# Two-layer decoder trunk: causal masks by GpSimd selects in two of three B groups, four output weights loaded during B, output projection in two halves, compact reciprocals

## The chip, the cores and the metric

The kernel runs on one core of a Trainium2 chip. TensorE (PE) multiplies, VectorE (DVE), ScalarE (ACT) and GpSimd (POOL) do the element-wise work, and DMA queues that SyncE (SP) and ACT issue move data. Each engine works through its own list of instructions in a fixed order; a scheduler wrote these lists when the program was built. The metric is the device time of one launch in microseconds (us).

## The reference

1024 prompt tokens and 32 sample tokens (8 sequences of 4) pass two layers of width 1024 in float32.

- Layer 0: one input projection gives queries, keys and values of an attention A (window 128) and of three dilated attentions B (groups g = 1, 2, 3 with window and dilation (128, 1), (512, 4), (2048, 16)), with 8 query heads on 2 key heads (`kv` = 0, 1), and a gate z. The three B groups share one softmax denominator. The result is `[A | B] * silu(z)`, then an output projection (1024 to 1024), the residual and a LayerNorm.
- Layer 1: mLSTM with 4 heads of 256, computed in chunks of 128 tokens, a gate, an output projection of the same kind, the residual and a LayerNorm.

```python
s = jnp.where(mask, s, NEG_INF)
p = jnp.exp(s - m[..., None]);  den = p.sum(-1)          # m, den joint over the three B groups
o = jnp.einsum('nbhgqk,nbkhd->nbqhgd', p, vv) / den
mix = concat([oa, ob]) * silu(z);  y = mix @ w_out       # 8 blocks of 128 input features, k = 0..7
out = layer_norm(DN_ALPHA * x + y, ln_g, ln_b)
```

## The kernel before

Every float32 product is made of three matmuls of rounded parts (high by high, high by low, low by high), so splits into a high part (ACT, `hi`) and a low part (DVE, `lo`) stand everywhere. The stages are: keys and values; queries woven with attention A and the maxima of B; the gate; **stage B** (`attention_b`, `samples`, `merges`, woven by `weave`); the output projection of layer 0 (`out0`, `out_proj`); layer 1 (`layer1`), which ends with the same `out_proj`.

In stage B, `scores` goes through blocks of 128 keys by 4 heads x 128 queries. A block of B is six matmuls of 512 columns before the change: the mask (identity times mask, `maskr`), two for the scores (`sc`), and three for the values (`av`: twice `ph`, once `pl`). ACT takes the exponential of `sc` twice, rounded (`ph`) and whole (`p`). `lo` makes `pl = p - ph`, on DVE, or on POOL for every fourth block (`POOL_LO`). For each kv there are 8 blocks of g = 3, then 12 of g = 2, then 15 of g = 1. When the last group has finished the queries of a chunk (`CH`: 384, 384 and 256 + 32 tokens), `OD` (65 rows: 64 values and the denominator) goes to DRAM.

`merge0(ty, kv, c)` reads it back, divides by the denominator, multiplies by the gate and splits into `M[c]` (`mh`, `ml`), the left side of the output projection: (0, 0) and (0, 1) are A and fill feature blocks k = 0 to 3, (1, 0) fills 4 and 5, (1, 1) fills 6 and 7. For (1, 1), which is the last, it reads the bare denominators to 64 partitions each and takes the reciprocal there (line 839); for the others `finish` has stored reciprocals.

The weights `wo0` come through the two `wraw` buffers (`load_wo`: load, `hi`, `lo`): k = 0, 1 at the end of `samples`, k = 2 to 7 in `out0`. The matmuls of the output projection are lines 163 to 165 (`py`).

Of the kernel before, what the change touches and what calls it, by code (L numbers as in the profile page):

```python
# [66 lines left out]
POOL_LO = 4  # L67

# [5 lines left out]
class Scratch:  # L74


    def __init__(self, *tiles):
        self.free = [[t, 0] for t in tiles]
        self.tags = {}

# [15 lines left out]
class Builder:  # L96
# [57 lines left out]
    def proj_tok(self, ps, i, X, xs, w):  # L154


        nc = self.nc
        for k in range(8):
# [289 lines left out]
    def scores(self, g, kv, hf, Q1, Q2, K1, K2, V, emit):  # L448
        nc = self.nc
        for qb in range(2 * hf, 2 * hf + 2):  # L450
# [4 lines left out]
            for bi, (kb, kind) in enumerate(bl):  # L455
# [11 lines left out]
                if g:  # L467
                    nc.scalar.activation(ph, sc, AF.Exp)
                    nc.scalar.activation(p, sc, AF.Exp)  # L469
                else:  # L470
                    nc.scalar.activation(p, sc, AF.Exp)
                    nc.gpsimd.affine_select(p, p, [[0, 4], [-1 if kind else 1, 128]], OP.is_ge, 0.0, base=0,
                                            channel_multiplier=1 if kind else -1)
                    self.hi(ph, p)
                pl = self.ppool.tile([128, 512], F32R, tag="pl", name="pl")
                if g and self.nsc % POOL_LO == 0:
                    nc.gpsimd.tensor_tensor(pl, p, f(ph), OP.subtract)
                else:
                    self.lo(pl, p, ph)
# [21 lines left out]
    def finish(self, ty, kv, sink_nm=None):  # L501
# [10 lines left out]
        self.store('m', self.FD[ty][kv].rearrange("h (b q) -> (h b) q", q=128), dn)  # L512

# [48 lines left out]
    def attn_b(self, kv, done=None):  # L562
# [253 lines left out]
    def merge0(self, ty, kv, c, M, inverse=True):  # L816
# [10 lines left out]
        OD = self.OD[ty][kv]  # L827
        D = self.FD[ty][kv] if inverse else OD[64]
        for u in range(2 * ty):
            pr = slice(64 * u, 64 * u + 64)  # L830
            self.load(o[pr, :, :m], OD[0:64].rearrange("d (c u) t -> d c u t", u=2)[:, :, u, t0:t0 + m])
            self.load(F[pr, :, :m], D.rearrange("(c u) t -> c u t", u=2)[:, u, t0:t0 + m].partition_broadcast(64))
# [29 lines left out]
    def out_proj(self, M, W, xres, g, b, consume, early={}):  # L862
        nc = self.nc
        with self.tc.tile_pool(name="lnp", bufs=3) as lp:
            for i in ORDER:
                m = 128 if i < 8 else 32
                if i == 6:
                    xs = self.pair(lp, M[2])
                xr = None
                if i in early:  # L870
                    r = early[i]
                else:
                    xr = lp.tile([128, 1024], F32, tag="xr", name="xr")
                    r = [xr[:, 0:512], xr[:, 512:1024]]
                    self.load(xr[:m], xres[128 * i:128 * i + m])
                for n in range(2):
                    ps = self.pp.tile([128, 512], F32, tag=("pj", "sc")[n], name="py")
                    ns = slice(512 * n, 512 * n + 512)
                    self.proj_tok(ps, i, M, xs if i == 8 else None, lambda k: [w[:, ns] for w in W[k]])
                    nc.vector.scalar_tensor_tensor(r[n][:m], r[n][:m], ALPHA, ps[:m], op0=OP.mult, op1=OP.add)  # L880
                    for c in (32,) if i == 8 else ():
                        nc.vector.tensor_tensor(r[n][:32], ps[c:c + 32], r[n][:32], OP.add)
                self.layer_norm(m, r, g, b)
                consume(i, m, r, xr)

    def layer0(self):
# [13 lines left out]
        self.FD = [[dt(f"FD{t}{i}", [4, TP]) for i in range(2)] for t in range(2)]  # L900
        self.SZ = dt("SZ", [8, 128, T])
# [9 lines left out]
        with tc.tile_pool(name="qp", bufs=2) as self.qp, tc.tile_pool(name="kp", bufs=2) as self.kp, \  # L911
# [46 lines left out]
            def last(c):  # L958
                if c < 2:
                    self.merge0(1, 1, c, self.M, False)  # L960
# [32 lines left out]
            def samples():  # L993
                sp = Scratch(*(self.x2p.tile([128, 3072], F32, tag=f"x{u}x2", name=f"scr{u}") for u in "hl"))
# [10 lines left out]
            self.merge0(1, 1, 2, M, False)  # L1005
# [3 lines left out]
    def out0(self):  # L1009
        nc, tc, A = self.nc, self.tc, self.A  # L1010
        M = self.M
        self.mp.release()
        with tc.tile_pool(name="wo", bufs=1) as wp:
            W = self.W0 + [self.load_wo(A['wo0'], k, *self.wo_tiles(wp, k)) for k in range(2, 8)]
            with tc.tile_pool(name="lnc", bufs=1) as lc:
                gb = [[lc.tile([128, 512], F32, name=f"ln{u}{c}") for c in range(2)] for u in "gb"]
                self.load_ln(0, gb)
                tags = (("x2", self.x2p), ("0", self.xp), ("1", self.xp))
# [142 lines left out]
    def proj_head(self, h):  # L1161
# [3 lines left out]
        else:  # L1165
            QT = self.hp.tile([128, 2, T], F32, tag="QT", name="QT", bufs=1)
        KT = self.hp.tile([128, 2, T], F32, tag="KTh", name="KTh")
# [201 lines left out]
    def layer1(self):  # L1369
# [3 lines left out]
        with tc.tile_pool(name="l1c", bufs=1) as lc:  # L1373
# [16 lines left out]
            with tc.tile_pool(name="hp", bufs=2) as self.hp:  # L1390
# [5 lines left out]
                with tc.tile_pool(name="ms", bufs=2) as self.ms:  # L1396
# [11 lines left out]
                    def load_m(c):  # L1408
                        tg, pool = (("x2", self.x2p), ("0", self.xp), ("2", self.xp))[c]
# [13 lines left out]
                    for k, t in ((2, "KTh"), (3, "QT")):  # L1423
                        x = self.hp.tile([128, 2, 1024], F32R, tag=t, name=f"o{k}", bufs=2 if k == 2 else 1)
# [51 lines left out]
    def body(self):  # L1476
        nc, tc = self.nc, self.tc
        with tc.tile_pool(name="dram", bufs=1, space=DRAM) as self.dram, \
# [20 lines left out]
            self.x2p.release()  # L1499

# [137 lines left out]
```

## Time and profile before

| | us |
|---|---|
| median of 3 runs | 1497.02 (1495.68 to 1500.87) |
| the profiled execution, whole | 1504.22 |
| its span in the profile | 1501.9 |
| PE busy in the span | 1416.9 (94%) |
| DVE, ACT, POOL busy | 896.6, 514.3, 203.1 |
| mean granted clock of PE in the span | 0.979 |

Times below are from the span's start. Stage B runs from about 485 to 656, the output projection of layer 0 to 765, and layer 1 follows. Matmuls are pipelined, so the distance between the starts of two of them tells what one costs, not its duration.

### The profile page before, as it was taken

The numbers are of one execution on the slowest core, as the hardware profiler recorded it, in microseconds if no ns is written. First come the engines' busy times: TensorE is split into PE (matmuls) and PEld (weight loads), VectorE is DVE, ScalarE is ACT, GpSimd is POOL, SyncE is SP. The second block draws the span as 40 slices with busy tenths as digits, with TensorE's granted clock in tenths as the row PEclk, the third lists the DMA queues.
The fourth block names the chain that finished last, engine by engine and source line by source line (L and its number), as shares of the span: only waits on it lengthen the run. The fifth ranks groups of instructions, "written<-read, shape, count | busy, mean of one in ns | idle before, by whom it ended". The sixth has DMA issues, their size and how long they took to land.

```text
span 1501.9 us, 22033 instructions
## 1 busy us (share of the span) xinstructions
PE 1416.9 (94%) x7862; PEld 1203.8 (80%) x7862; DVE 896.6 (60%) x2480; ACT 514.3 (34%) x939; POOL 203.1 (14%) x249
## 2 busy tenths in 40 slices
PE   8999999998899898879999999999999999998997
PEld 8989999898898544457788878988898899877785
DVE  5312457577576756669774535655565566566786
ACT  5332254542123756721133313331333133333310
POOL 1002243422321212101000000100000000000010
PEclk9999999999999989989999999999999999999999
DMA  8446565556753789564222655364323322341741
GB/s 297 168 143 196 176 194 163 173 160 178 198 172 98 234 254 246 171 200 122 96 79 76 216 198 204 105 194 131 77 78 117 117 49 69 117 129 23 241 138 46
DMA packets 139306, 226.85 MB, mean 151 GB/s; under 512 B 17216, under 2 KB 107296, under 8 KB 138680
## 3 DMA queue, kind: packets, MB, share of 16 engines
q1 hardware_dynamic: 129496, 201.96, 44.0%
q10 hardware_dynamic: 9702, 23.50, 4.5%
q8 instruction: 62, 1.02, 0.3%
q14 instruction: 46, 0.38, 0.1%
HBM read 166.60 MB, written 81.88 MB: 165 GB/s over the span
## 4 chain that ended last, share of the span: by engine, by line
PE 69%; DMA 16%; DVE 8%; issue 4%; ACT 2%; SPq 1%; POOL 0%; DVEq 0%; ACTq 0%; POOLq 0%
PE pj L197 10%; PE pj L199 10%; PE pj L198 10%; PE py L163 3%; PE py L165 3%; PE py L164 3%; PE pvo L163 3%; PE pvo L164 3%; PE pvo L165 3%; DMA G<-GR 2%; DMA OD<-OD 1%; DMA K<-KK 1%; PE st L431 1%; DMA wr<-in_wo_dram 1%; DMA out_cmems_dram<-Cs 1%
## 5 line engine op out<-in xcount | busy, mean ns | idle before, releaser
L197 PE MATMUL pj<-xh,wh 128*128 128x384 f32 (+1 forms) x576 | 189.1, 328 | 8.4 <-DVE sz L609 3.3
L197 PE MATMUL pj<-x1h,wh 128*128 128x384 f32 (+1 forms) x576 | 189.3, 329 | 1.7 <-ACT QT L1171 1.6
L199 PE MATMUL pj<-xh,wl 128*128 128x384 f32 (+1 forms) x576 | 188.4, 327 | 0.0
L198 PE MATMUL pj<-xl,wh 128*128 128x384 f32 (+1 forms) x576 | 188.3, 327 | 0.0
L199 PE MATMUL pj<-x1h,wl 128*128 128x384 f32 (+1 forms) x576 | 187.6, 326 | 0.0
L198 PE MATMUL pj<-x1l,wh 128*128 128x384 f32 (+1 forms) x576 | 187.3, 325 | 0.0
L197 PEld LDWEIGHTS pj<-xh,wh 128*128 128x128 f32 x576 | 110.4, 192 | 12.6 <-DVE sz L609 4.3
L197 PEld LDWEIGHTS pj<-x1h,wh 128*128 128x128 f32 x576 | 108.3, 188 | 6.5 <-issue 3.3
L199 PEld LDWEIGHTS pj<-x1h,wl 128*128 128x128 f32 x576 | 108.3, 188 | 6.0 <-issue 5.8
L198 PEld LDWEIGHTS pj<-x1l,wh 128*128 128x128 f32 x576 | 108.4, 188 | 4.0 <-issue 3.8
L198 PEld LDWEIGHTS pj<-xl,wh 128*128 128x128 f32 x576 | 110.3, 191 | 1.6
L199 PEld LDWEIGHTS pj<-xh,wl 128*128 128x128 f32 x576 | 110.3, 192 | 0.9
L435 DVE CUSTOM_DVE_ANT_0 junk<-st,maskr 128x256 f32<-128x256 f32 (+1 forms) x256 | 93.0, 363 | 26.7 <-PE st L431 9.5
L163 PE MATMUL pvo<-voh,x1h 128*128 128x512 f32 x256 | 102.3, 402 | 3.0 <-DVE SZ L1187 3.0
L164 PE MATMUL pvo<-voh,x1l 128*128 128x512 f32 x256 | 101.4, 399 | 0.0
L165 PE MATMUL pvo<-vol,x1h 128*128 128x512 f32 x256 | 100.6, 396 | 0.0
L808 POOL TENSOR_TENSOR rsw<-rsw,mhalf 128x1 f32<-128x1 f32 (+1 forms) x54 | 40.1, 743 | 318.7 <-DVE rsw L807 303.5
L114 DVE TENSOR_TENSOR pl<-p,ph 128x512 fp32r<-128x512 f32 x82 | 63.6, 782 | 29.0 <-ACT p L469 16.6
L110 ACT ACTIVATE wh<-wr 128x1024 fp32r<-128x1024 f32 x48 | 50.7, 1057 | 75.9 <-PE pj L198 69.9
L120 POOL TENSOR_TENSOR wl<-wr,wh 128x1024 fp32r<-128x1024 f32 x24 | 58.0, 2415 | 131.1 <-ACT qs L231 70.6
L431 PE MATMUL st<-K,QZ 128*128 128x256 f32 x256 | 52.1, 292 | 10.7 <-DMA QZ<-QQ 5.6
L163 PEld LDWEIGHTS pvo<-voh,x1h 128*128 128x128 f32 x256 | 48.8, 191 | 13.8 <-DVE SZ L1187 3.3
(352 smaller groups left out, 3165.1 us busy)
## 6 DMA issues: line engine op xcount, KB each, us to landing
Q<-QQ SPq DMA_DIRECT2D x32, 512.0 KB
out_kvs_dram<-in_cache_b_kv_dram SPq DMA_DIRECT2D x16, 1022.0 KB
wr<-in_w0f_dram SPq DMA_DIRECT2D x24, 512.0 KB
wr<-in_w1f_dram SPq DMA_DIRECT2D x24, 512.0 KB
QQ<-sh ACTq DMA_DIRECT2D x16, 512.0 KB
QQ<-sl ACTq DMA_DIRECT2D x16, 512.0 KB
QZ<-QQ SPq DMA_DIRECT2D x32, 256.0 KB
wr<-in_wo_dram SPq DMA_DIRECT2D x16, 512.0 KB
```

What stands on the lines that cost most here:

```text
L110: return self.nc.scalar.activation(out, in_, AF.Copy, scale=scale)
L114: return self.nc.vector.tensor_tensor(out, in_, f(hi), OP.subtract)
L120: self.nc.gpsimd.tensor_tensor(out, in_, f(hi), OP.subtract)
L163: nc.tensor.matmul(ps, xh[:, k, t], wh, start=k == 0, stop=False)
L164: nc.tensor.matmul(ps, xl[:, k, t], wh, start=False, stop=False)
L165: nc.tensor.matmul(ps, xh[:, k, t], wl, start=False, stop=k == 7)
L197: nc.tensor.matmul(ps[:, :n], wh[:, k, :], xh[:, k, :n], start=k == 0, stop=False)
L198: nc.tensor.matmul(ps[:, :n], wh[:, k, :], xl[:, k, :n], start=False, stop=False)
L199: nc.tensor.matmul(ps[:, :n], wl[:, k, :], xh[:, k, :n], start=False, stop=k == 7)
L431: nc.tensor.matmul(st[:, u, :], Q1[:, h, q0:q0 + 128], K1[:, w0:w0 + 256], start=True, stop=True)
L435: nc.vector.tensor_tensor_reduce(junk[:, :n], st[:, u, c0:c0 + n], mk, 1.0, -3e38, OP.add, OP.max, ST[:, 8 * h + qb:8 * h + qb + 1])
L808: nc.gpsimd.tensor_tensor(r, v, self.mhalf[:m], OP.pow)
```

## The change

In g = 1 and g = 2 the mask matmul goes; POOL zeroes the masked half after the exponential (`affine_select`, as attention A does already), and ACT copies the result to `ph`. `POOL_LO` goes, so every `pl` is made on DVE. For (1, 1) a new `finish_chunk` loads the denominators of a chunk as 12 (or 8) rows of 128, takes the reciprocal there, stores it (`FDC`), and `merge0` reads that back and multiplies on POOL as for the others. `samples` loads four output weights instead of two, the new ones into the buffers that it has finished with, and some tiles of layer 1 move with these buffers. `out_proj` gives the first two token tiles their PSUM together and contracts k = 0 to 3 of both ahead of k = 4 to 7.

```diff
@@ scores
-                if g:
-                    mk = self.maskr[:, 256:384] if g == 3 else self.maskr[:, 128 - 128 * kind:256 - 128 * kind]
-                    nc.tensor.matmul(so, mk, self.identr.unsqueeze(1).to_broadcast([128, 4, 128]), start=True, stop=False)
-                nc.tensor.matmul(so, K1[:, ks], Q1[:, :, q0:q0 + 128], start=not g, stop=False)
+                if g == 3:
+                    nc.tensor.matmul(so, self.maskr[:, 256:384], self.identr.unsqueeze(1).to_broadcast([128, 4, 128]), start=True, stop=False)
+                nc.tensor.matmul(so, K1[:, ks], Q1[:, :, q0:q0 + 128], start=g < 3, stop=False)
...
-                if g:
+                if g == 3:
                     nc.scalar.activation(ph, sc, AF.Exp)
                     nc.scalar.activation(p, sc, AF.Exp)
                 else:
...
-                if g and self.nsc % POOL_LO == 0:
-                    nc.gpsimd.tensor_tensor(pl, p, f(ph), OP.subtract)
-                else:
-                    self.lo(pl, p, ph)
+                self.lo(pl, p, ph)
@@ new
+    def finish_chunk(self, c):
+        n = 4 * (min(CH[c][1], TP - CH[c][0]) // 128)
+        dn = self.mp.tile([128, 2, 384], F32, tag="mf", name="dnc")[:, 0, 0:128]
+        self.store('m', dn[:n], self.ODC[c][64].rearrange("h (b q) -> (h b) q", q=128))
+        self.nc.vector.reciprocal(dn[:n], dn[:n])
+        self.store('m', self.FDC[c].rearrange("h (b q) -> (h b) q", q=128), dn[:n])
@@ attn_b
-                    self.store('b', self.OD[1][kv][:, :, t], OD[:, :, t])
+                    self.store('b', self.ODC[qb // 3] if kv else self.OD[1][kv][:, :, t], OD[:, :, t])
@@ merge0
-            if inverse:
-                nc.gpsimd.tensor_tensor(o[:, :, :m], o[:, :, :m], F[:, :, :m], OP.mult)
-            else:
-                for a in range(2):
-                    nc.vector.reciprocal(F[:, a, :m], F[:, a, :m])
-                nc.vector.tensor_tensor(o[:, :, :m], o[:, :, :m], F[:, :, :m], OP.mult)
+            nc.gpsimd.tensor_tensor(o[:, :, :m], o[:, :, :m], F[:, :, :m], OP.mult)
@@ out_proj
-            for i in ORDER:
+            for grp in (ORDER[:2],) + tuple((i,) for i in ORDER[2:]):
+                parts = (range(4), range(4, 8)) if len(grp) > 1 else (range(8),)
...
@@ samples
-                for k in range(2):
-                    w = [self.wsp.tile([128, 1024], F32R, tag=f"w{u}", name=f"o{u}") for u in "hl"]
+                for k in range(4):
+                    if k < 2:
+                        w = [self.wsp.tile([128, 1024], F32R, tag=f"w{u}", name=f"o{u}") for u in "hl"]
+                    else:
+                        x = self.x2p.tile([128, 2, 1024], F32R, tag=f"x{'bc'[k - 2]}", name="ox")
+                        w = [x[:, 0, :], x[:, 1, :]]
```

What the scheduler makes of it shows at three places. First PE, near the end of stage B (g = 1, kv = 1). The number after a name is its buffer, and rises from block to block; `av` with `ph_6346` is the first value matmul of the block whose scores went to the `sc` before 6376.

```order
L462 MATMUL sc_6376<-identr_951,maskr_949 128x512
L463 MATMUL sc_6376<-Q1_6370,K1_6140 128x512
L464 MATMUL sc_6376<-Q2_6372,K2_6141 128x512
L483 MATMUL av_6327<-pl_6336,V_6146 66x512
L481 MATMUL av_6327<-ph_6346,V_6146 66x512
L482 MATMUL av_6327<-ph_6346,V_6146 64x512
```

That is the order before, where the values of a block come right behind the scores of the next one. The order of the changed kernel at the same place:

```order
L465 MATMUL sc_6387<-Q1_6381,K1_6147 128x512
L466 MATMUL sc_6387<-Q2_6383,K2_6148 128x512
L485 MATMUL av_6308<-pl_6317,V_6153 66x512
L483 MATMUL av_6308<-ph_6326,V_6153 66x512
L484 MATMUL av_6308<-ph_6326,V_6153 64x512
```

Here `ph_6326` belongs to the scores `sc_6322`; `sc_6337`, `sc_6350` and `sc_6387` stand between them and these values, so PE has two to three further blocks scored where it had one.

Second DVE, at the first reciprocal for (1, 1), chunk 0. `av_6202` holds the last queries of chunk 0; two more sums into `OD` stand between it and line 839, which works on 128 rows (`x2` is two of them):

```order
L576 TENSOR_TENSOR OD_5661<-av_6202,OD_5661 65x4x128
L114 TENSOR_TENSOR pl_6308<-p_6304,ph_6305 128x512
L576 TENSOR_TENSOR OD_5661<-av_6245,OD_5661 65x4x128
L114 TENSOR_TENSOR pl_6321<-p_6317,ph_6318 128x512
L114 TENSOR_TENSOR pl_6336<-p_6332,ph_6333 128x512
L576 TENSOR_TENSOR OD_5661<-av_6299,OD_5661 65x4x128
L839 RECIPROCAL mf_6232<-mf_6232 128x384 x2
L114 TENSOR_TENSOR pl_6384<-p_6380,ph_6381 128x512
```

In the changed kernel the reciprocal is on 12 rows (line 517). The last queries of chunk 0 are `av_6209`, and one sum stands between; six `pl` of stage B follow line 517 where four followed line 839:

```order
L582 TENSOR_TENSOR OD_5668<-av_6209,OD_5668 65x4x128
L116 TENSOR_TENSOR pl_6276<-p_6271,ph_6272 128x512
L582 TENSOR_TENSOR OD_5668<-av_6254,OD_5668 65x4x128
L116 TENSOR_TENSOR pl_6317<-p_6312,ph_6313 128x512
L116 TENSOR_TENSOR pl_6330<-p_6325,ph_6326 128x512
L517 RECIPROCAL dnc_6238<-dnc_6238 12x128
L116 TENSOR_TENSOR pl_6345<-p_6340,ph_6341 128x512
```

Third POOL, at the multiply of (1, 0), chunk 0, in the middle of stage B. Before, one block in four had an instruction on POOL, and the multiply stood between two of these:

```order
L477 TENSOR_TENSOR pl_5751<-p_5747,ph_5748 128x512
L836 TENSOR_TENSOR mo_5695<-mo_5695,mf_5696 128x768
L477 TENSOR_TENSOR pl_5838<-p_5834,ph_5835 128x512
L391 MEMSET K2_6141 1x1024
L400 MEMSET V_6146 128x8x2
```

In the changed kernel the selects of all blocks of g = 1 and 2 stand in that list, behind the same multiplies and memsets:

```order
L473 AFFINE_SELECT p_5652<-p_5652 128x512
L402 MEMSET V_5876 128x8x2
L393 MEMSET K2_6148 1x1024
L843 TENSOR_TENSOR mo_5702<-mo_5702,mf_5703 128x768
L473 AFFINE_SELECT p_5888<-p_5888 128x512
L402 MEMSET V_6153 128x8x2
```

From the gates of layer 1 on, the order on PE is the same in both programs. At the output projection both programs contract the first two token tiles side by side, k after k.

## Rows read from the trace of the kernel before

**Rows 1.** Busy time by stage, from the windows: B, its end, projection, rest.

```profile
core 0: us, PE busy (x) PEld busy (x) DVE busy (x) ACT busy (x) POOL busy (x), PEclk, DMA share, GB/s
485.00:631.60 146.60, 128.75 (x645) 73.80 (x645) 99.30 (x175) 97.74 (x178) 30.18 (x27) 0.92 0.77 229
631.60:642.10 10.50, 9.71 (x42) 6.23 (x40) 3.45 (x5) 8.40 (x15) 2.35 (x2) 1.00 0.62 153
642.10:684.70 42.60, 29.65 (x106) 21.57 (x105) 33.15 (x32) 10.39 (x12) 2.48 (x1) 0.88 0.62 190
684.70:1494.00 809.30, 790.00 (x4396) 672.11 (x4396) 493.23 (x1517) 225.58 (x463) 47.50 (x127) 1.00 0.39 119
```

**Rows 2.** Timeline of PE: start, duration, and in brackets the idle time before.

```profile
637.35 0.39 PE L462 MATMUL sc<-identr,maskr 128*128 128x512 f32 x1
637.58 0.40 PE L463 MATMUL sc<-Q,K 128*128 128x512 f32 x1
...
648.56 0.69 PE L483 MATMUL av<-pl,V 128*66 128x512 f32 x1 [4.92 <-DVE pl L114]
...
667.15 0.50 PE L163 MATMUL py<-oh,mh 128*128 128x512 f32 x1 [3.13 <-ACT oh L110]
...
675.64 0.50 PE L163 MATMUL py<-oh,mh 128*128 128x512 f32 x1 [1.11 <-ACT oh L110]
...
679.98 0.50 PE L165 MATMUL py<-ol,mh 128*128 128x512 f32 x1 [2.23 <-DVE ol L114]
```

**Rows 3.** Timeline of DVE at the reciprocals of chunk 0.

```profile
643.00 4.96 DVE L839 RECIPROCAL mf<-mf 128x384 f32<-128x384 f32 x2 [4.76 <-DMA mf<-OD]
```

**Rows 4.** Chain that ended last, 485 to 685: shares by line, and pieces.

```profile
by line: issue 10.3%; DMA OD<-OD 6.8%; PE av L481 5.0%; DMA mz<-SZ 4.4%; PE sc L464 4.4%; PE sc L462 4.3%; PE av L483 4.2%; DMA KT<-in_vc_dram 4.1%; DMA K<-KK 4.1%; PE av L482 4.0%; DMA mf<-OD 3.9%; PE sc L463 3.8%; DMA wr<-in_wo_dram 3.6%;
```

**Rows 5.** The same chain, pieces in order of time: start, length, what.

```profile
475.10 2.28 DMA NMB<-NM
...
631.60 4.29 DMA OD<-OD
...
637.90 5.01 DMA mf<-OD
...
660.82 7.17 DMA wr<-in_wo_dram
```

**Rows 6.** Groups by form, 485 to 690: count, busy and mean ns, idle before.

```profile
L114 DVE TENSOR_TENSOR pl<-p,ph 128x512 fp32r<-128x512 f32 x50 | 35.4, 715 | 11.5 <-ACT p L469 11.5
L511 DVE RECIPROCAL dn<-dn 32x128 f32<-32x128 f32 x1 | 0.9, 914 | 0.0
L469 ACT ACTIVATE p<-sc 128x512 f32<-128x512 f32 x66 | 38.6, 591 | 0.0
L110 ACT ACTIVATE oh<-wr 128x1024 fp32r<-128x1024 f32 x8 | 8.4, 1056 | 17.0 <-DMA wr<-in_wo_dram 12.9 <-PE av L483 2.2 <-PE so L728 1.9
L462 PE MATMUL sc<-identr,maskr 128*128 128x512 f32 x64 | 28.6, 447 | 0.7 <-ACT p L469 0.7
L477 POOL TENSOR_TENSOR pl<-p,ph 128x512 fp32r<-128x512 f32 x17 | 24.1, 1416 | 103.0 <-ACT p L469 88.3 <-PE sc L463 14.6
L836 POOL TENSOR_TENSOR mo<-mo,mf 128x768 f32<-128x768 f32 x2 | 3.9, 1968 | 13.6 <-DMA mf<-FD 13.6
L400 POOL MEMSET V<- 128x16 f32 x4 | 0.5, 114 | 10.0 <-PE av L483 10.0
```

**Rows 7.** Groups by form in attention A, 200 to 322.

```profile
L472 POOL TENSOR_SCALAR_AFFINE_SELECT p<-p 128x512 f32<-128x512 f32 x30 | 25.6, 866 | 30.2 <-ACT p L471 30.2
L110 ACT ACTIVATE ph<-p 128x512 fp32r<-128x512 f32 x30 | 18.5, 632 | 5.1 <-PE av L482 3.6 <-POOL p L472 0.8
```

**Rows 8.** Timelines of POOL and DVE in attention A: two selects, one low part.

```profile
278.32 0.64 POOL L472 TENSOR_SCALAR_AFFINE_SELECT p<-p 128x512 f32<-128x512 f32 x1 [7.15 <-ACT p L471]
...
313.61 1.06 POOL L472 TENSOR_SCALAR_AFFINE_SELECT p<-p 128x512 f32<-128x512 f32 x1 [3.01 <-ACT p L471]
...
313.49 0.68 DVE L114 TENSOR_TENSOR pl<-p,ph 128x512 fp32r<-128x512 f32 x1
```

More of the change, by code (lines that the diff above doesn't have):

```diff
@@ L79, in __init__, with home @@
         self.tags = {}
+    def home(self, x):
+        return [t.tensor for t, _ in self.free].index(x.tensor)
     def tile(self, shape, dt, tag=None, name=None):
@@ L152, in pair, with proj_tok @@
         return xs
-    def proj_tok(self, ps, i, X, xs, w):
+    def proj_tok(self, ps, i, X, xs, w, ks=range(8)):
         nc = self.nc
-        for k in range(8):
+        for k in ks:
             wh, wl = w(k)
@@ L864, in out_proj @@
         with self.tc.tile_pool(name="lnp", bufs=3) as lp:
-            for i in ORDER:
[L866 to L884, printed above, removed]
+            for grp in (ORDER[:2],) + tuple((i,) for i in ORDER[2:]):
+                parts = (range(4), range(4, 8)) if len(grp) > 1 else (range(8),)
+                todo = []
+                for i in grp:
+                    m = 128 if i < 8 else 32
+                    if i == 6:
+                        xs = self.pair(lp, M[2])
+                    xr = None
+                    if i in early:
+                        r = early[i]
+                    else:
+                        xr = lp.tile([128, 1024], F32, tag="xr", name="xr")
+                        r = [xr[:, 0:512], xr[:, 512:1024]]
+                        self.load(xr[:m], xres[128 * i:128 * i + m])
+                    todo.append((i, m, r, xr, [self.pp.tile([128, 512], F32, tag=("pj", "sc")[n], name="py")
+                                               for n in range(2)]))
+                for ks in parts:
+                    for i, m, r, xr, ps in todo:
+                        for n in range(2):
+                            ns = slice(512 * n, 512 * n + 512)
+                            self.proj_tok(ps[n], i, M, xs if i == 8 else None, lambda k: [w[:, ns] for w in W[k]], ks)
+                            if ks[-1] < 7:
+                                continue
+                            nc.vector.scalar_tensor_tensor(r[n][:m], r[n][:m], ALPHA, ps[n][:m], op0=OP.mult, op1=OP.add)
+                            for c in (32,) if i == 8 else ():
+                                nc.vector.tensor_tensor(r[n][:32], ps[n][c:c + 32], r[n][:32], OP.add)
+                        if ks[-1] == 7:
+                            self.layer_norm(m, r, g, b)
+                            consume(i, m, r, xr)
@@ L900, in layer0 @@
         self.FD = [[dt(f"FD{t}{i}", [4, TP]) for i in range(2)] for t in range(2)]
+        self.ODC = [dt(f"ODC{c}", [65, 4, min(n, TP - t0)]) for c, (t0, n) in enumerate(CH)]
+        self.FDC = [dt(f"FDC{c}", [4, min(n, TP - t0)]) for c, (t0, n) in enumerate(CH)]
         self.SZ = dt("SZ", [8, 128, T])
@@ L993, in samples @@
             def samples():
-                sp = Scratch(*(self.x2p.tile([128, 3072], F32, tag=f"x{u}x2", name=f"scr{u}") for u in "hl"))
+                sp = Scratch(*(self.x2p.tile([128, 2 * T], F32, tag=f"x{u}", name=f"scr{u}") for u in "abc"))
                 yield from self.sample_attn(sp)
-                for k in range(2):
-                    w = [self.wsp.tile([128, 1024], F32R, tag=f"w{u}", name=f"o{u}") for u in "hl"]
+                assert sp.home(self.OS) == 0
+                for k in range(4):
+                    if k < 2:
+                        w = [self.wsp.tile([128, 1024], F32R, tag=f"w{u}", name=f"o{u}") for u in "hl"]
+                    else:
+                        x = self.x2p.tile([128, 2, 1024], F32R, tag=f"x{'bc'[k - 2]}", name="ox")
+                        w = [x[:, 0, :], x[:, 1, :]]
                     self.W0.append(self.load_wo(A['wo0'], k, *w))
@@ L1012, in out0 @@
         self.mp.release()
+        self.x1p = tc.alloc_tile_pool(name="x1p", bufs=1)
         with tc.tile_pool(name="wo", bufs=1) as wp:
-            W = self.W0 + [self.load_wo(A['wo0'], k, *self.wo_tiles(wp, k)) for k in range(2, 8)]
+            W = self.W0 + [self.load_wo(A['wo0'], k, *self.wo_tiles(wp, k)) for k in range(4, 8)]
             with tc.tile_pool(name="lnc", bufs=1) as lc:
@@ L1422, in layer1 @@
                                                              for u in "hl")))
-                    for k, t in ((2, "KTh"), (3, "QT")):
-                        x = self.hp.tile([128, 2, 1024], F32R, tag=t, name=f"o{k}", bufs=2 if k == 2 else 1)
+                    for k, t in ((2, "xb"), (3, "xa")):
+                        x = self.x2p.tile([128, 2, 1024], F32R, tag=t, name=f"o{k}")
                         W.append(self.load_wo(A['wo1'], k, x[:, 0, :], x[:, 1, :]))
@@ L1499, in body @@
             self.x2p.release()
+            self.x1p.release()
 def arrays(inp):
```

25 lines of the change are left out of this document (13 added, 12 removed).

## The prediction

> **What bounds the kernel now.** I read the windows first [rows 1]. From 684.7 to 1494 the columns show PE busy for 790 of 809 us at a granted clock of 1.00 (2.4 GHz): whatever reaches 684.7 earlier ends earlier by as much, since from the gates on PE's order is the same. Before that, PE does not bind. In stage B (485 to 631.6) the clock is 0.92, so part of the stage has the lower level (1.2 GHz), and the DMA engines are busy for 0.77; in the end of B (642.1 to 684.7) PE has 106 matmuls in 42.6 us. What one costs when nothing waits is the distance of two starts, 0.23 us [rows 2]: 106 x 0.23 = 24.4 us, so 18.2 us are lost there. The brackets of PE's timeline say on what: 4.92 us for low parts on DVE, then 3.13, 1.11 and 2.23 us for the parts of output weights [rows 2]. DVE was late with the low parts because it stood for 4.76 us before the reciprocals, waiting for the denominators, and then worked 4.96 us on them [rows 3]. The chain agrees: store of OD, its read, later a load of weights of 7.17 us [rows 5].
>
> **Mask matmuls.** For each kv, 27 of 35 blocks lose one: 54 x 0.23 = 12.4 us of PE work. It is worth that only where PE is on the chain. The chain from 485 to 685 holds line 462 for 4.3% of 200 us, 8.6 us [rows 4]; of the 64 matmuls recorded there [rows 6] all but about ten go, so some 7.3 us. PE sees nothing else removed.
>
> **Selects.** The block's path grows. Before, ACT's exponential (0.59) gives the rounded values at once; now exponential 0.59 [rows 6], select 0.64 when alone [rows 8], 0.87 on average, and copy 0.63 [rows 7]: 1.3 to 1.5 us more per block. I cost this at nothing, because PE's new order has two to three blocks scored ahead where it had one, and each block is five matmuls, 1.15 us; without that cover it would be 54 x 1.3 = 70 us. ACT still has two instructions per block, so its work stays.
>
> The select does collide with DVE. A low part that ran from 313.49 to 314.17 met a select that began at 313.61 and lasted 1.06 us: it ends at 314.67, about a lone select's 0.64 after the low part [rows 8]. So the two take turns, 0.64 + 0.69 = 1.33 us per block, against 1.38 for six matmuls before. If that sets the pace of the 54 blocks, they gain 54 x 0.05 = 2.7 us; if PE sets it, 12.4. I take 5, nearer to the lower end and under the chain's 7.3, as both selects and low parts are in every block.
>
> The Trainium skill has the rule to this (SBUF — State Buffer, "SBUF: two separate sides"): DVE and GpSimd share a pair of SBUF ports as an exclusive lock, held for a whole instruction, if the DVE instruction reads two SBUF inputs. The rows agree, 1.06 against 0.64. Taken alone it would put the gain of this part at 2.7 instead of 12.4; it is the second rival's rule.
>
> **Low parts moved to DVE.** The 17 instructions of POOL (1.42 each) become 17 to 18 of 0.72 on DVE [rows 6]: 12.5 us more for an engine that is busy for 99.3 of 146.6 us [rows 1]. The idle third covers it: 0. Without cover, 12.5.
>
> **Two weights earlier.** Two loads of 512 KB at 229 GB/s [rows 1] are 4.6 us of DMA time in a stage with DMA share 0.77; their high parts are 2 x 1.06 on ACT [rows 6], the low parts about as much on DVE. Idle time covers nearly all; I take -1 (0 to -4.6). In the end of B it leaves four weights to split, not six, and 48 matmuls rather than 24 that need neither the last merges nor late weights: 24 x 0.23 = 5.5 us more to fill waits with.
>
> **Two halves.** Both orders contract the first two tiles k after k, so this edit alone gives 0. The moved tiles of layer 1 give 0 too: same order, PE busy.
>
> **Compact reciprocals and the end of B.** I lay the new chain from the store of chunk 0 (631.60 before): store 4.29, small load like the 2.28, reciprocal 0.91, small store 2.28, broadcast read 5.01, multiply 1.97 on POOL [rows 5, 6]: 16.7 us. Before, the reciprocals ended at 647.96 [rows 3], 16.4 after the store. The chain is no shorter; what shrinks is DVE's hold, 4.96 to 0.91. It still waits for store and small load (6.6 us, less some 2.5 of work ahead of it), with six low parts behind. Chunk 1 uses the same buffer (`mf`, one), so it follows by 2.28 + 0.91 + 2.28 + 5.01 + 1.97 = 12.5: 29.2. ACT's split of chunk 1 stands ahead of the last two weights in the new order: some 2 us for gate and split, 2 x 1.06 for the weights, 33.3; the last 24 matmuls of two tiles 5.5: done at about 39 after the store. Before, that was at 684.7, 53.1 after it. Gain 14; less 3, as the new order places the store some two blocks later in the work. I take +11 (+5 to +16); by lost time, it leaves 7 of the 18.2 us.
>
> **Sum.** 5 + 0 - 1 + 11 = 15 us. Against the profiled execution's 1504.2 that is 1489; the median of the runs is 7.2 lower, so I put 1482 for it.
>
> **Rivals.**
> *PE sets the pace throughout* (0.17). Masks 12.4, and the waits of short lead go with the longer one; the stage's clock of 0.92 is 12 us of 146.6, of which I give it 4. 12.4 + 4 - 1 + 11 = 26: 1471. For it: the order. Against: share 0.77 of DMA.
> *The ports or DVE set the pace* (0.15). 12.5 us of low parts, and each of 54 waits half a select (0.32): 17 us. DVE would be at (99.3 + 12.5 + 17) / 146.6 = 0.88 in an order that is fixed: by estimate a third of the 17 us is not absorbed, and stage B is 6 us slower. -6 - 1 + 11 = 4: 1493. The rule of the shared ports decides it.
> *DMA sets the pace of B* (0.10). Then the masks give nothing and the weights cost 4.6: 11 - 4.6 = 6: 1491. For it: K, V and cache pieces on the chain [rows 4], 4.1% each.
> *Slower: the selects stand in POOL's queue behind what waits* (0.08). Multiplies waited 13.6 us for their data, V's memsets 10.0 us for PE [rows 6]. Before, one block in four stood behind; now all. If all 23.6 us reach PE, 5 - 1 - 23.6 + 11 = -8.6: 1506. It decides when more than 15 of the 23.6 us do. Against: the eight blocks of g = 3 need no select and stand beside the first multiply.
>
> **How the numbers follow.** The forecast has 0.50, its own range 1475 to 1489 (masks 2.7 to 12.4, end 5 to 16, not all together). 0.3% is 4.5 us here, about what a measurement can tell from no change. Faster than 1492.5: forecast, first and third rival, and a third of the second: 0.50 + 0.17 + 0.10 + 0.05 = 0.82. Within 0.3%: most of the rest of the second, 0.10. Slower: the fourth, 0.08. The range for 8 in 10 leaves out the fourth (0.08), the lowest third of the first (0.06) and the upper third of the second (0.05): 1465 to 1495.
>
> **What would show it.** Right: line 462's form falls to 16 matmuls; where g = 1 is dense, scores of neighbouring blocks stand about 1.2 to 1.35 us apart, not 1.4; the wait of 4.92 us before a value matmul shrinks to under 4; the second token tile is done within 40 us of the store of chunk 0; the rest takes 809 us as before. Wrong: selects of 1.0 us and more on average with PE waiting for `ph` (ports); long waits on POOL before line 843 with PE idle (queue); a stage after 690 that changes its length, for which I have no term; or PE waiting for weights k = 6, 7 for more than 5 us, if the second chunk's denominators come late.

## The result and the profile after

| | us |
|---|---|
| before, median of 4 runs | 1498.35 (1495.68 to 1500.87) |
| changed, median of 4 runs | 1486.97 (1484.69 to 1489.61) |
| ratio | 0.9928 (95%: 0.9905 to 0.9952) |
| changed, the profiled execution, whole and span | 1484.69, 1483.0 |

The change saves 10.8 us (7 to 14). The two profiled executions stand 18.9 us apart, which is more than the medians: before's was a long one, the changed kernel's a short one. So single stretches are compared with care below. How far two executions of one program differ is seen in experiment 4: spans of 1483.0 and 1491.6.

The windows of the changed kernel, cut at its store of chunk 0 (632.4, before 631.6), at its first matmul of the output projection, and where the third token tile starts (671.7, before 684.7; compare [rows 1]):

```profile
core 0: us, PE busy (x) PEld busy (x) DVE busy (x) ACT busy (x) POOL busy (x), PEclk, DMA share, GB/s
485.00:632.40 147.40, 123.52 (x598) 65.85 (x597) 109.61 (x192) 101.70 (x180) 55.18 (x59) 0.87 0.80 232
632.40:642.30 9.90, 6.92 (x28) 3.86 (x27) 6.12 (x10) 7.36 (x14) 4.15 (x6) 1.00 0.30 81
642.30:671.70 29.40, 24.94 (x107) 18.84 (x106) 15.97 (x21) 7.95 (x10) 4.85 (x4) 1.00 0.72 220
671.70:1475.00 803.30, 788.94 (x4396) 671.73 (x4396) 493.14 (x1519) 226.21 (x464) 48.54 (x128) 1.00 0.38 122
```

The store comes no earlier: PE is busy for 5 us less in the first window, but the window is as long. From the store to the third tile it takes 39.3 us where it took 53.1. Here the gain is seen. The rest took 803 us, not 809, with the same matmuls; of the edits only the moved tiles of layer 1 stand there, and I put no gain on it. Over the fourteen profiled executions of this document, the part from the first transpose (`trx`) to the end takes 789.8 to 798.8 us: 798.8 in before, 791.9 and 794.6 in two executions of the changed program, and 794.5 in experiment 5, where no tile of layer 1 moves.

Two things can make a stretch shorter: PE waits less, or the same matmuls take less of its time because the granted clock is higher. The next windows separate them (columns as above). First stage B, of before, the changed kernel, and experiments 6 (mask matmuls and selects) and 7 (neither); then the stretch from the last score matmul of B to the first transpose, of before, the changed kernel, and experiment 4 (the changed program a second time); last six us of before, behind its wait of 4.92 us [rows 2]:

```profile
483.10:641.10 158.00, 139.36 (x693) 81.34 (x693) 104.65 (x182) 105.30 (x191) 32.53 (x28) 0.92 0.76 225
481.70:641.00 159.30, 132.60 (x638) 71.79 (x638) 117.72 (x203) 109.45 (x193) 58.28 (x64) 0.88 0.77 223
479.30:640.20 160.90, 138.88 (x693) 80.71 (x692) 116.56 (x202) 109.66 (x193) 60.84 (x64) 0.93 0.75 221
482.70:630.20 147.50, 127.22 (x639) 70.36 (x639) 113.95 (x199) 107.51 (x193) 10.76 (x12) 0.91 0.81 238
...
641.35:703.18 61.83, 48.88 (x190) 37.14 (x188) 49.05 (x70) 12.36 (x16) 5.75 (x4) 0.92 0.51 151
641.28:691.11 49.83, 45.21 (x195) 35.22 (x194) 33.06 (x61) 11.03 (x15) 9.80 (x9) 1.00 0.56 172
643.51:696.99 53.48, 48.76 (x194) 38.48 (x193) 35.05 (x69) 10.90 (x15) 12.40 (x10) 0.91 0.57 178
...
648.50:654.50 6.00, 5.94 (x14) 4.37 (x15) 4.62 (x7) 1.93 (x3) 2.48 (x1) 0.50 0.25 67
```

Behind stage B, PE's idle time (the window less the busy time) falls from 13.0 us to 4.6, and to 4.7 in experiment 4: some 8.3 us of waits are gone in both executions. The other 3.7 us of the 12.0 are PE's busy time, at a clock of 1.00 where before had 0.92. Experiment 4's execution had 0.91 with the same lists and is busy as long as before, so this part comes and goes from one execution to the next; of before only one execution has a profile.

The chain that ended last shows the new path at the end of stage B, step by step (start, length, what; compare [rows 5]):

```profile
632.41 4.19 DMA ODC<-OD
636.67 1.54 DMA dnc<-ODC
638.30 0.95 DVE dnc L517
639.26 1.91 DMA FDC<-dnc
641.88 3.95 DMA mf<-FDC
645.96 1.85 POOL mo L843
...
658.43 1.84 POOL mo L843
```

And PE's timeline, its waits there (compare [rows 2]):

```profile
628.98 0.46 PE L464 MATMUL sc<-Q,K 128*128 128x512 f32 x1
...
630.20 0.39 PE L464 MATMUL sc<-Q,K 128*128 128x512 f32 x1
...
631.38 0.40 PE L464 MATMUL sc<-Q,K 128*128 128x512 f32 x1
...
639.84 0.45 PE L481 MATMUL av<-pl,V 128*66 128x512 f32 x1 [1.92 <-DVE pl L116]
...
663.13 0.50 PE L165 MATMUL py<-oh,mh 128*128 128x512 f32 x1 [1.13 <-ACT oh L112]
...
668.68 0.39 PE L167 MATMUL py<-ol,mh 128*128 128x512 f32 x1
...
671.69 0.50 PE L165 MATMUL py<-oh,mh 128*128 128x512 f32 x1 [2.62 <-DVE xr L892]
```

The wait for low parts behind the reciprocals is 1.92 us, where it was 4.92; those for parts of weights are down to 1.13. Two tiles are done at 669.07, 36.7 us after the store. Then a wait stands that was 0.78 before: the third tile waits 2.62 us until DVE, which has a merge of chunk 2 to do first, has emptied the PSUM of the first tile.

In stage B the waits have a new name. Groups by form, 485 to 640 (compare [rows 6, 7]):

```profile
L473 POOL TENSOR_SCALAR_AFFINE_SELECT p<-p 128x512 f32<-128x512 f32 x51 | 47.6, 943 | 46.3 <-ACT p L472 45.0 <-DMA KT<-in_kt_dram 1.1
L116 DVE TENSOR_TENSOR pl<-p,ph 128x512 fp32r<-128x512 f32 x62 | 43.4, 715 | 9.2 <-ACT ph L112 8.8 <-ACT p L470 0.4
L112 ACT ACTIVATE ph<-p 128x512 fp32r<-128x512 f32 x51 | 31.2, 625 | 11.9 <-POOL p L473 11.6 <-PE av L480 0.2
```

A select takes 0.94 us on average, and ACT waits 11.6 us in front of its copies for it: 0.23 each on average, but five waits of 1.6 to 2.1 us are 9.2 of it. While ACT waits, the copy and the exponentials of later blocks wait in its queue. One of the five, and PE's value matmul behind it:

```profile
591.24 1.22 ACT L112 ACTIVATE ph<-p 128x512 fp32r<-128x512 f32 x2 [1.59 <-POOL p L473]
...
591.92 0.69 PE L479 MATMUL av<-ph,V 128*66 128x512 f32 x1 [1.04 <-ACT ph L112]
```

So leaving out 12.4 us of mask matmuls did not shorten stage B in the profile. By the windows, about half came back as busy time at a lower clock and the rest as waits: 55 recorded matmuls fewer are some 12.7 us at 0.23, but PE's busy time falls by 6.8 us only, at a clock of 0.88 for 0.92, and its idle time rises from 18.6 us to 26.7.

### The profile page after: what moved, and what is told of

It is laid out like the page before. It is cut to its first block, busy times and chain, and to the rows that moved or that the text cites. A ratio compares the mean times of both kernels' runs of the same rounds, so it can differ in the third digit from the quotient of the medians.

```text
span 1483.0 us, 21926 instructions
## 1 busy us (share of the span) xinstructions
PE 1402.2 (95%) x7808; PEld 1188.4 (80%) x7808; DVE 893.3 (60%) x2492; ACT 516.5 (35%) x939; POOL 231.5 (16%) x288
## 4 chain that ended last, share of the span: by engine, by line
PE 67%; DMA 17%; DVE 8%; issue 3%; ACT 2%; SPq 1%; POOL 1%; DVEq 0%; ACTq 0%; POOLq 0%
PE pj L199 10%; PE pj L201 10%; PE pj L200 10%; PE py L165 3%; PE py L167 3%; PE py L166 3%; PE pvo L165 3%; PE pvo L166 3%; PE pvo L167 3%; DMA G<-GR 1%; DMA Q<-QQ 1%; DMA K<-KK 1%; DMA OD<-OD 1%; DMA out_cmems_dram<-Cs 1%; DVE junk L437 1%
## 5 line engine op out<-in xcount | busy, mean ns | idle before, releaser
L200 PEld LDWEIGHTS pj<-xl,wh 128*128 128x128 f32 x576 | 109.6, 190 | 1.6
L116 DVE TENSOR_TENSOR pl<-p,ph 128x512 fp32r<-128x512 f32 x100 | 77.2, 785 | 27.5 <-ACT ph L112 22.9
L473 POOL TENSOR_SCALAR_AFFINE_SELECT p<-p 128x512 f32<-128x512 f32 x84 | 75.9, 915 | 82.8 <-ACT p L472 81.3
```

The source lines that it names most:

```text
L116: return self.nc.vector.tensor_tensor(out, in_, f(hi), OP.subtract)
L200: nc.tensor.matmul(ps[:, :n], wh[:, k, :], xl[:, k, :n], start=False, stop=False)
```

## The experiments

Times beside "before" are differences from it: (ratio - 1) x 1498. The intervals of the ratios are 0.2 to 0.4% wide to each side, 3 to 6 us. "Stage B" is the distance, in the one profiled execution, from the last projection matmul of 384 columns (`pj<-xl,wh`, line 198 of before) to the first of the two score matmuls of B's last block; "end" is from there to the first transpose of the first LayerNorm's result (`trx`).

| | ratio (95%) | us | stage B | end |
|---|---|---|---|---|
| before | 1 | 0 | 158.0 | 62.1 |
| changed | 0.9928 (0.9905, 0.9952) | -10.8 | 159.4 | 50.1 |
| 1 masks back | 0.9950 (0.9931, 0.9968) | -7.5 | 161.3 | 51.0 |
| 2 selects alone | 0.9970 (0.9948, 0.9992) | -4.5 | 154.4 | 65.6 |
| 3 old reciprocals | 1.0003 (0.9984, 1.0021) | +0.4 | 155.9 | 66.4 |
| 4 the changed kernel again | 0.9913 (0.9889, 0.9936) | -13.0 | 160.8 | 53.8 |
| 5 reciprocals alone | 0.9982 (0.9964, 1.0000) | -2.7 | 156.1 | 58.3 |
| 6 both masks | 0.9939 (0.9917, 0.9960) | -9.1 | 160.9 | 51.4 |
| 7 no select | 0.9847 (0.9809, 0.9885) | -22.9 | 147.5 | 55.2 |
| 8 unmasked | 0.9852 (0.9822, 0.9883) | -22.2 | 154.2 | 49.8 |
| 9 small select | 0.9899 (0.9882, 0.9915) | -15.1 | 155.8 | 52.6 |
| 10 alternate | 0.9995 (0.9978, 1.0013) | -0.7 | 170.2 | 59.4 |
| 11 late last merges | 0.9912 (0.9887, 0.9937) | -13.2 | 156.1 | 48.0 |
| 12 four buffers for p | 0.9925 (0.9898, 0.9952) | -11.2 | 168.2 | 49.6 |

**1. The masks by matmul again.** `scores` as before, all else changed:

```diff
-                if g == 3:
+                if g:
+                    mk = self.maskr[:, 256:384] if g == 3 else self.maskr[:, 128 - 128 * kind:256 - 128 * kind]
...
-                self.lo(pl, p, ph)
+                if g and self.nsc % POOL_LO == 0:
+                    nc.gpsimd.tensor_tensor(pl, p, f(ph), OP.subtract)
+                else:
+                    self.lo(pl, p, ph)
```

> The changed kernel with the mask matmuls of g = 1 and 2 back in place of the selects (and one low part in four back on GpSimd); all else stays changed. Theory 1 (from the two traces: the scores of stage B end at 641.1 in both, so the 12.4 us of matmuls came back as waits): within 3 us of the changed kernel's 1487, between 1484 and 1490. Theory 2 (the forecast: masks worth 5): 1492. Theory 3 (PE sets the pace of stage B): 12 slower, 1499.

Measured -7.5: 3.3 slower than the changed kernel, 5.5 than its repetition. Theory 3 falls; 1 and 2 can't be told apart by this run, and the other side of it helps:

**2. The selects alone**, in the kernel before (the diff of `scores` and no other).

> The kernel before with the selects alone: no mask matmuls in g = 1 and 2, no low part of B on GpSimd; old reciprocals, two early weights, old loop of the projection. Theory 1 (selects pay nothing): 1495 to 1501 beside 1498 of before. Theory 2: 1493. Theory 3: 1486, as fast as the whole change.

-4.5. Two pairs of kernels that differ by this edit alone give 4.5, and 3.3 or 5.5. My reading of the two traces, that it pays nothing, was that of one execution each; the edit pays about 4 us, each value known to 3 us or so.

**3. The old reciprocals** in the changed kernel.

```diff
-                self.finish_chunk(c)
...
-            nc.gpsimd.tensor_tensor(o[:, :, :m], o[:, :, :m], F[:, :, :m], OP.mult)
+            if kv:
+                for a in range(2):
+                    nc.vector.reciprocal(F[:, a, :m], F[:, a, :m])
+                nc.vector.tensor_tensor(o[:, :, :m], o[:, :, :m], F[:, :, :m], OP.mult)
+            else:
+                nc.gpsimd.tensor_tensor(o[:, :, :m], o[:, :, :m], F[:, :, :m], OP.mult)
```

> The changed kernel with the old reciprocals for (1, 1): bare denominators read to 64 partitions each, reciprocal of 128 x 384 twice on DVE. Theory A (the gain at the end of stage B is that of DVE's shorter hold): the wait of some 5 us before a value matmul at 640 to 650 comes back, 1492 to 1498. Theory B (it comes from the two weights that are split earlier): 1487 to 1489, since 48 matmuls of the projection fill the wait.

The whole gain is gone, Theory A by its time. But the wait is not where A had put it. PE's timeline shows it at the weights:

```profile
655.22 0.76 PE L165 MATMUL py<-oh,mh 128*128 128x512 f32 x1 [3.25 <-ACT oh L112]
...
676.17 0.80 PE L165 MATMUL py<-oh,mh 128*128 128x512 f32 x1 [9.25 <-ACT oh L112]
```

The low parts of the values are no longer waited for; the order has the longer lead. The trace's chain behind the 9.25 us goes another way, through the buffers of the weights:

```profile
659.37 1.28 DVE mf L845
...
661.78 2.29 DVE ol L116 x2
...
664.76 10.28 DMA wr<-in_wo_dram
675.07 1.06 ACT oh L112
```

The reciprocals of chunk 1 hold DVE from 656.90 to 661.86, and the low parts of two weights stand behind them. These low parts read the two `wraw` buffers, which are free only behind them; the loads of the last two weights go out at 664.76, and ACT can split the first of them at 675.07. In the changed kernel these loads go out at 656.65 and 658.34.

**4. The early weights undone, as I thought.** Weights 2 and 3 are asked for in `out0`, into the same two buffers.

```diff
-                for k in range(4):
+                for k in range(2):
...
+            for k in (2, 3):
+                x = self.x2p.tile([128, 2, 1024], F32R, tag=f"x{'bc'[k - 2]}", name="ox")
+                W.append(self.load_wo(A['wo0'], k, x[:, 0, :], x[:, 1, :]))
```

> The changed kernel with only weights k = 0 and 1 loaded during stage B; k = 2 and 3 go to the same buffers, but are loaded in the projection's own part, as before. Theory A (the gain at the end is that of the reciprocals): 1487 to 1489. Theory B (it comes from the two weights): the waits for parts of weights between 655 and 685 come back, 6.5 us in the profile of before, so 1493 to 1496.

The scheduler took the loads forward again: but for line numbers, the lists of all five engines are those of the changed kernel. So this run measures the changed kernel a second time (-13.0 beside -10.8) and says nothing of the weights. The place of the call does not bring them early; what is left is their buffers, which no run changes alone.

**5. The compact reciprocals alone**, in the kernel before (`finish_chunk`, chunk stores, `merge0`).

> The kernel before with the compact reciprocals alone: chunk stores, line 517's reciprocal on 12 rows, multiply on GpSimd; mask matmuls, two early weights and everything else as before. Theory A (the gain of the whole change is that of the reciprocals, 11 by the forecast's end of stage B): 1486 to 1490 beside 1498 to 1499 of before. Theory B (they need the longer lead of the selects or the early weights to pay): 1493 to 1499.

-2.7, Theory B. With the early weights beside them (experiment 1) it is -7.5. PE's timeline says where it went:

```profile
648.53 0.50 PE L163 MATMUL py<-oh,mh 128*128 128x512 f32 x1 [3.43 <-DVE OD L584]
...
659.07 0.50 PE L163 MATMUL py<-oh,mh 128*128 128x512 f32 x1 [3.31 <-ACT oh L110]
...
669.68 0.50 PE L163 MATMUL py<-oh,mh 128*128 128x512 f32 x1 [3.22 <-ACT oh L110]
```

and ACT's says what the splits waited for:

```profile
657.96 1.06 ACT L110 ACTIVATE oh<-wr 128x1024 fp32r<-128x1024 f32 x1 [9.98 <-DMA wr<-in_wo_dram]
...
668.57 1.06 ACT L110 ACTIVATE oh<-wr 128x1024 fp32r<-128x1024 f32 x1 [6.85 <-DMA wr<-in_wo_dram]
```

The low parts are no longer waited for; PE arrives earlier at weights that have not landed yet, and at sums of DVE (3.43 us, and 2.37 before the third tile).

**6. Both masks**: mask matmuls in all groups, and the selects stay.

```diff
-                if g == 3:
+                if g:
+                    mk = self.maskr[:, 256:384] if g == 3 else self.maskr[:, 128 - 128 * kind:256 - 128 * kind]
```

> The changed kernel with the mask matmuls of g = 1 and 2 added again, while the selects stay: each block is masked twice, PE has 54 matmuls or 12.4 us more work, and nothing else changes but the order that the scheduler gives. Theory 1 (PE has that much idle time in stage B, so a mask matmul costs little): 1487 to 1490. Theory 3 (PE sets the pace): 1499.

-9.1: 12.4 us more PE work cost 1.7 to 3.9. That is Theory 1 by the time, but idle time is only part of it. The windows show PE's busy time in stage B at 138.9 us, 6.3 more than in the changed kernel (3.7 more than in experiment 4's execution), since the clock is 0.93, not 0.88 or 0.87; its idle time falls by some 4 us. With the mask matmuls PE has more to do and does it at a higher clock.

**7. No select**: the select goes for g = 1 and 2, the copy to `ph` stays (first piece). **8. Unmasked**: all groups take the two exponentials of g = 3 (second piece). Both leave the masks out, and so compute something else than the reference.

```diff
+                    if not g:
                         nc.gpsimd.affine_select(p, p, [[0, 4], [-1 if kind else 1, 128]], OP.is_ge, 0.0, base=0,
...
-                if g == 3:
+                if g:
                     nc.scalar.activation(ph, sc, AF.Exp)
                     nc.scalar.activation(p, sc, AF.Exp)
```

> The changed kernel without the selects of g = 1 and 2, and without mask matmuls: those blocks stay unmasked (left out). ACT still makes the rounded part by a copy of the exponential, so its work and the long lead stay. Theory P (the shared ports and the select's share of a block's path ate the 12.4 us): 1477 to 1481. Theory D (transfers and ACT set the pace of stage B, whatever POOL does): 1484 to 1488.

> The changed kernel without selects and without mask matmuls in g = 1 and 2 (masks left out), and with ACT's two exponentials as for g = 3: the rounded part does not wait for the copy, and the scheduler gives the short lead again. The shortest possible path of a block. Theory P: 1475 to 1480. Theory D: 1484 to 1488, as without the selects alone. If the copy's wait is what costs, it is under e7 by 3 or more.

-22.9 and -22.2, Theory P: the selects cost the changed kernel 10 to 12 us (each of the two values known to 4 to 6). In 7 stage B is 147.5 us long, 11.9 shorter: by the windows, 6.4 us of idle time and 5.4 of busy time, at a clock of 0.91 for 0.88. In 8, which has the short lead again, it is 154.2. DMA does not set the pace. No cost of ACT's copy by itself is seen (8 is no faster than 7), though 3 us could hide in the noise. In 7, the copies wait for no select:

```profile
L112 ACT ACTIVATE ph<-p 128x512 fp32r<-128x512 f32 x54 | 32.0, 623 | 2.0 <-PE av L481 1.1 <-ACT ph L112 0.6 <-ACT p L472 0.2
```

**9. A small select**: its length, or the step?

```diff
+                    ps, hs = (p[:, 0:128], 1) if g else (p, 4)
-                    nc.gpsimd.affine_select(p, p, [[0, 4], [-1 if kind else 1, 128]], OP.is_ge, 0.0, base=0,
+                    nc.gpsimd.affine_select(ps, ps, [[0, hs], [-1 if kind else 1, 128]], OP.is_ge, 0.0, base=0,
```

> The changed kernel with the selects of g = 1 and 2 cut to 128 of 512 columns (one of four heads; the other three stay unmasked, left out). Every block still has a GpSimd instruction between the exponential and ACT's copy. Theory L (what costs is the select's length, 0.64 us alone and 0.98 us when a low part runs on DVE): near the kernel without selects, 1476 to 1481. Theory H (any step through GpSimd costs, whatever its length): 1483 to 1488, as the changed kernel.

-15.1, between the two: of 10 to 12 us, 2 to 4 go with three quarters of the columns (which stay unmasked here), some 8 stay. The groups of this run show why both theories were too simple:

```profile
L474 POOL TENSOR_SCALAR_AFFINE_SELECT p<-p 128x128 f32<-128x128 f32 x51 | 28.3, 558 | 66.8 <-ACT p L472 66.1 <-DMA Q<-QQ 0.4
L112 ACT ACTIVATE ph<-p 128x512 fp32r<-128x512 f32 x51 | 31.3, 624 | 14.3 <-POOL p L474 11.7 <-DVE pl L116 1.4 <-PE av L481 1.0
```

ACT waits 11.7 us for the short selects, as for the long ones. Alone one takes 0.29 us (18 of the 37 that stand singly in POOL's timeline from 485 to 645, each with no low part on DVE over it), the other 19 take 0.67 on average: that time goes by waiting for DVE. Other selects wait before they start. ACT's longest wait is for one that stood behind a multiply in POOL's queue:

```profile
591.14 3.03 POOL L844 TENSOR_TENSOR mo<-mo,mf 128x768 f32<-128x768 f32 x1 [1.17 <-DMA mf<-FD]
...
594.45 0.63 ACT L112 ACTIVATE ph<-p 128x512 fp32r<-128x512 f32 x1 [3.16 <-POOL p L474]
```

How much of the 8 us is DVE, how much POOL's queue and how much the step through another engine, no run here separates.

**10. Every second block by select**; the others take mask matmul and two exponentials.

```diff
+                mm = g == 3 or (g and self.nsc % 2)
-                if g == 3:
+                if mm:
```

> The changed kernel with selects in every second block of g = 1 and 2 and mask matmuls in the others: 27 mask matmuls, 6.2 us, return to PE, 27 selects leave the path. Theory 1 with L (PE has idle time, selects make ACT wait 11.6 us in stage B): half of these waits go at little cost, 1481 to 1485. Theory 3 (PE sets the pace): 1490 to 1494.

The middle way lost everything, and neither theory had it. In the groups, ACT waits more for 21 recorded selects than for 51:

```profile
L112 ACT ACTIVATE ph<-p 128x512 fp32r<-128x512 f32 x21 | 13.1, 625 | 14.3 <-POOL p L475 12.4 <-DVE scrc L698 1.8
```

In the order that the scheduler gives this program, PE has mostly one or two further blocks scored ahead of a block's values; in the changed kernel it is two or three. ACT waits 0.59 us for each select. That the shorter lead is the cause is argued from this order; no run changes the lead alone.

**11. The last merges late.** Chunk 2's merges, which the first six tiles don't need, get a lower priority.

```diff
-            self.merge0(1, 1, 2, M)
-            run(merges((2,)))
+            with tc.high_priority(-400):
+                self.merge0(1, 1, 2, M)
+                run(merges((2,)))
```

> The changed kernel with the last merges (chunk 2) given a lower priority, so that on DVE the sums of the first two token tiles (line 892) stand ahead of them. Theory: in the changed kernel PE waited 2.62 us for that sum before the third tile; this wait goes and the rest stays, 1484 to 1485. Rival: the third tile then waits for something else, or the later chunk 2 makes the last tiles wait: 1487 or more.

The 2.62 us wait is gone from PE's timeline; between 642 and 690 the longest is this one, and one other of over 0.5 us stands there, 0.88 at 683.94:

```profile
657.42 0.50 PE L165 MATMUL py<-oh,mh 128*128 128x512 f32 x1 [1.13 <-ACT oh L112]
```

The ratio is 0.9912, beside 0.9928 and 0.9913 of the changed kernel: a gain of 2 us can't be told from none here.

**12. Four buffers for p**, two for `pl`, and the late merges.

> The changed kernel with four buffers for the exponential p where it had three, two for its low part pl where it had three (the same memory), and the late last merges of the run before. ACT can then run one more exponential ahead of a copy that waits for its select. Theory: ACT's 11.6 us of waiting for selects in stage B, 0.23 us per copy, fall to under 8, and with the 2.6 us of the late merges the time is 1478 to 1482. Rival: the wait moves to DVE or PE, since two low parts now bound the lead; then only the late merges show, 1484 to 1487.

ACT's wait for selects fell to 6.5 us, as the theory had it, but the time is that of the rival. The scheduler also moved work between the stages, and a wait of 5.67 us stands at the start of stage B:

```profile
L112 ACT ACTIVATE ph<-p 128x512 fp32r<-128x512 f32 x53 | 32.8, 624 | 10.7 <-POOL p L473 6.5 <-DVE scra L767 2.6 <-DVE pl L116 1.5
```

```profile
494.46 0.69 PE L479 MATMUL av<-ph,V 128*66 128x512 f32 x1 [5.67 <-DVE OD L580]
```

No version tried here that computes the reference beats the changed kernel by more than the runs can tell.

## Why the prediction was right, point by point

The forecast was 15 us less, 1482; measured are 10.8 and, in experiment 4, 13.0. It lies in the forecast's own range of 1475 to 1489.

- **Masks, 5.** Measured 4.5, and 3.3 or 5.5. The size was right, one step was not: "I cost this at nothing", of the longer path of a block. The lead hides the path from most of PE's values, but not from ACT's queue, where the copy stands ahead of later exponentials. Without the selects the part is worth 15.4 (experiment 7 against 1), near the 12.4 + 4 that the first rival gave it; with them, 4. So the nearness of the 5 is in part luck: a larger gain and a cost of 10 to 12 us, which the sum did not have, leave about as much. The sum also left the clock of stage B as it was, and it fell. The turn-taking with DVE is seen: of the 31 selects that stand singly in POOL's timeline from 485 to 645, the nine that met no low part took 0.64 us each, the 22 others 0.98. One of each kind, and the two low parts around the longer one:

```profile
617.48 1.20 POOL L473 TENSOR_SCALAR_AFFINE_SELECT p<-p 128x512 f32<-128x512 f32 x1 [1.66 <-ACT p L472]
...
636.85 0.64 POOL L473 TENSOR_SCALAR_AFFINE_SELECT p<-p 128x512 f32<-128x512 f32 x1 [0.30 <-ACT p L472]
```

```profile
616.96 1.23 DVE L116 TENSOR_TENSOR ox<-wr,ox 128x1024 fp32r<-128x1024 f32 x1 [0.74 <-ACT ox L112]
618.10 1.12 DVE L116 TENSOR_TENSOR pl<-p,ph 128x512 fp32r<-128x512 f32 x1
```

The first low part (of a weight) ended at 618.19, the select at 618.68; the second low part began before that and ended at 619.22, after 1.12 us where a lone one takes 0.68. So both sides are held up: seven of the 31 low parts that met a select between 485 and 645 took 1.00 to 1.12. The average of 0.715 does not show it, as before had a few that met POOL's own instructions (up to 1.40) in its 0.715 [rows 6]. The Trainium skill (SBUF — State Buffer, "SBUF: two separate sides") says that whichever of the two starts first holds the shared ports for its whole instruction, and the other is blocked; the trace agrees in both directions. But the price in the prediction was too high: the one held up ends 0.49 to 0.54 us after the other, not a whole 0.64 or 0.69 later, and the rows that it read say the same (314.17 to 314.67, 0.50 [rows 8]). Where the two alternate at 628.95, 629.95 and 630.95, selects start 1.00 us apart, less than five matmuls (1.15), so the 1.33 us per block and the 2.7 us drawn from it do not hold.

- **Low parts on DVE, 0.** No run undoes this alone. DVE is busy for 109.6 of 147.4 us, so idle time to cover them was there.
- **Two halves, 0.** The changed program built with the old loop of `out_proj` has, but for buffer numbers, the same list on every engine.
- **Two weights, -1.** Open. With the compact reciprocals they bring 4.8 (experiment 1 against 5), with the old ones they cost 4.9 (3 against 2), each with some 4 us of uncertainty. That the compact reciprocals need them is seen in experiment 5's waits for weights; a kernel with selects and compact reciprocals and without them was not run.
- **End of B, 11.** The terms were 4.29, 2.28, 0.91, 2.28, 5.01, 1.97; the chain shows 4.19, 1.54, 0.95, 1.91, 3.95, 1.85: 15.4 for 16.7, the second chunk at 27.9 for 29.2, two tiles at 36.7 for 39. From the store to the third tile it is 13.8 us less than before. That the gain needs the reciprocals is shown by experiment 3, which loses 11.2 by undoing them. Two things were not in the sum. One is the next wait, the third tile's 2.62 us. The other is the clock: the prediction read all of the 18.2 lost us as waits, but its brackets come to 11.4, and behind the wait of 4.92 us the kernel before ran for six us at 0.50 (the last window above), the level of 1.2 GHz. In the changed kernel's profile no part of this stretch runs below 1.00; in experiment 4's some does. So some 8.3 us of the gain at this end are waits, which the sum is made of, and up to 3.7 the clock.
- **The rivals.** PE's pace throughout falls by experiment 6, DMA's pace by 7. The ports' rival falls by the time (it had 1493), though the turns that it counted are there. POOL's queue is seen too, with ACT waiting in front of its copy, and far from the 23.6 us that this rival reckoned with: 1.89 us behind a multiply that itself had waited for data, and 1.68 behind a memset of 1.81:

```profile
604.35 1.80 POOL L843 TENSOR_TENSOR mo<-mo,mf 128x768 f32<-128x768 f32 x1 [4.88 <-DMA mf<-FD]
...
606.77 0.63 ACT L112 ACTIVATE ph<-p 128x512 fp32r<-128x512 f32 x1 [1.89 <-POOL p L473]
```

- **Signs named in advance.** The masks went; blocks of g = 1 stand 1.18 to 1.22 us apart (628.98, 630.20, 631.38), at the lower end of what was named; the wait is under 4, and the tiles are done within 40. One sign failed: the rest took 803 us, not 809. A length of the later part that changes stood among the signs of being wrong, with no term for it; the spread over fourteen executions is wider than this, so it decides nothing.

## What to carry to other kernels

An instruction that moves to an idle engine is not free because that engine is idle: look at what waits in whose queue between the two halves of the step, and cost the hold there, per instruction, and with what stands ahead of the step in the idle engine's own queue. Matmuls that are taken away do not all come off the busy time: read the granted clock beside it, since here half of them came back at a lower clock. Edits to one chain do not add: the same reciprocals were worth 2.7 us with late weights and 11 in the changed kernel, since each only moves PE to the next wait. And where a scheduler decides, compare the lists before measuring an edit: one of these edits changed nothing, one experiment was the same program, and two that looked like improvements reordered the rest.

## What the runs showed that I had not expected

- A select of a quarter of the columns is barely waited for less: 11.7 us of ACT's time where the full one has 11.6, as 19 of 37 single ones took 0.67 instead of 0.29 us with a low part on DVE, and others stood behind POOL's multiplies and memsets.
- Halving the number of selects made the kernel 0.7% slower (0.9995 against 0.9928).
- The mask matmuls were half free: with them the granted clock is higher. Not only the profiles show it. The mean granted clock of a whole launch, averaged over all runs, is 0.981 to 0.984 in the four programs with mask matmuls in every block of B (before, 1, 5, 6) and 0.977 to 0.979 where selects stand in their place in all blocks of g = 1 and 2 (changed and its repetition 4, and 2 and 3). Some 0.004 of 1490 us is 6 us, by estimate, of 12.4. Without selects and masks (7, 8) it is 0.981 and 0.982, so the missing matmuls alone do not explain it.
- Two executions of the same program differ by 3.7 us in the end of stage B, 50.1 and 53.8, and the difference is the clock: PE is busy for 45.2 us at 1.00 in one and for 48.8 us at 0.91 in the other, with the same idle time.
